# Loading and gating the attention half's output weights before the state-space half's out-projection, in other buffers

## The chip, the cores and the metric

The kernel runs on one core of one Trainium2 chip. The metric is the device time of one launch in microseconds. The kernel before took 1314.43 us (median of three runs, 1313.91 to 1320.89). A change is told from no change here from about 0.5% on, which is 6.6 us.

## The reference, cut to what matters

One decoder layer on 1024 positions of 1024 channels. The input projection is split into two groups of 512 channels: stick-breaking attention (8 heads of 64) and a state-space part. Both are normalised, put side by side, and sent through one output projection:

```python
o = concat([rmsnorm(o_attn, attn_out_g), rmsnorm(o_ssm, ssm_out_g)], axis=-1)
x = x + g1 * (o @ w_out)            # w_out: 1024 x 1024
h = modulate(rmsnorm(x, norm2_g), sh2, sc2)
up = causal_dwconv(h @ ffn_w_up)    # 1024 x 5632, width 3
val, gate = split(up, 2)
x = x + g2 * ((gelu(gate) * val) @ ffn_w_down)
```

The first 512 rows of `w_out` belong to attention, the last 512 to the state-space part.

## The kernel before

Products are done in float32 as three matmuls: each operand is split into a rounded `hi` and a rest `lo`, and hi·hi, hi·lo and lo·hi are summed. The work has four stages: adaLN, norm and input projections with the state-space scan (to about 316 us); attention (to about 579 us); the rest of the output projection and the second norm (to about 690 us); the gated MLP (to the end).

**Attention.** `head` works through the query blocks of a head. A block needs TensorE for the scores (`z`), ScalarE for two sigmoids (`nb`, `sig`), VectorE for a scan over `nb` (L733), GpSimd for a product (`sig`), TensorE for transposes (`wT`), ScalarE and VectorE for the split into `wh` and `wl`, and TensorE for the product with v (`ops`), summed into `oT`. Heads 0 to 5 run one after the other; heads 6 and 7 alternate in groups of two blocks, the last blocks first.

**Fillers.** Beside the heads, two generators are moved on step by step: `ada_fill` (the rest of adaLN, tiles `adps`, `ada_raw`) and `fill`. `marks` holds the places at which `fill` makes a step, as shares of the total work of the heads (a block i counts i + 2, a head 44, all heads 352). The last two heads begin at 0.75, and what is left of `fill` is then run at once. `fill` does, in this order: weight tiles 0 and 1 of the state-space half, the norm statistics of the state-space output (`ssm_stats`, from `oS`), weight tiles 2 and 3, then eight times `ssm_out` (one block of 128 positions), then the four weight tiles of the attention half.

`wout_tile` makes one weight tile: a load of 512 KB into `raw` (tile `woraw`), a VectorE product with the norm gain and `g1row` (the gating), and on GpSimd the rounding to `wohi` and the subtraction to `wolo`. There are four `wohi` and four `wolo` buffers, so that a tile of the attention half can be rounded only when the state-space half has read its own tile for the last time.

`ssm_out` loads a block of x into a tile with the tag `x1`, runs 24 matmuls (two halves of 512 columns, four weight tiles, three products; L806 to L808, tile `wops`), adds the result (L67) and stores the block to `x1_d`. The tag `x1` has one buffer. `woraw`, `ssm_out`'s x and the throw-away output `junk2` of the second norm all use it, so each waits for the one before.

**Tail.** `load_xacc` reads the eight blocks back from `x1_d`: blocks 0 to 3 into the two buffers of the tag `qkraw`, blocks 4 to 7 into the buffer of `oS`. `tail_stats(g)` takes the attention output's statistics as each pair of blocks is complete, and `tail_proj` does the 24 matmuls per block with the attention half's weights, the sum, and the statistics of the second norm. Eight blocks make 192 matmuls. The second norm's transposes (`norm2_t`) and the first MLP products follow.

**Order.** The program gives priorities by its own order. A planner with a cost model then sets each engine's order and takes an instruction when it reckons that its operands and buffers are there. On the chip each engine, and each engine's DMA queue, runs its list in that fixed order and waits at the head of it.

Of the kernel before, what the change touches and what calls it, by code (L numbers as in the profile page):

```python
# [9 lines left out]
F32 = mybir.dt.float32  # L10
# [25 lines left out]
def hybrid_layer_kernel(  # L36
# [17 lines left out]
    act, dve, pool, pe, sp = nc.scalar, nc.vector, nc.gpsimd, nc.tensor, nc.sync  # L54

    def alloc(name, side="left", bufs=1, space=None):
        kw = {} if space is None else {"space": space}
        return tc.alloc_tile_pool(name=name, bufs=bufs, side=side, reuse_waits="tile", **kw)

    def tt(eng, out, a, b, op):  # L60
        eng.tensor_tensor(out=out, in0=a, in1=b, op=op)  # L61
# [4 lines left out]
    def stt(out, a, s, b, op0, op1):  # L66
        dve.scalar_tensor_tensor(out=out, in0=a, scalar=s, in1=b, op0=op0, op1=op1)  # L67
# [108 lines left out]
    def pool_round(o, i):  # L176
        pool.tensor_scalar(out=o, in0=i, scalar1=1.0, scalar2=0.0, op0=MUL, op1=ADD)  # L177
# [37 lines left out]
    for k in range(NK):  # L215
# [4 lines left out]
        raw = ada_raw[k]  # L220
# [177 lines left out]
    for i, (tab, k0) in enumerate(((rot[0], 0), (rot[1], 4))):  # L398
        pool.memset(tab[:, 0, :, 0:1], 1.0)
        pool.memset(tab[:, 1, :, 0:1], 0.0)  # L400
        for k in range(4 - i):
            n = 1 << k
# [215 lines left out]
    for cix in range(2):  # L618
        his, los = load_wchunk(cix)
        for tq in range(4):  # L620
# [14 lines left out]
            for j in range(2):  # L635
# [13 lines left out]
                for r in range(2):  # L649
                    act.dma_start(out=qk_d[cix, r].rearrange("(a p) t -> p a t", p=128)[:, :, t * 128:(t + 1) * 128],  # L650
                                 in_=hl[:, r].bitcast(F32).rearrange("p (a t) -> p a t", t=128))
    smb.release()
    sm.release()
    xq = alloc("qkraw", side="right")
# [31 lines left out]
    osp = alloc("oprep", side="right", bufs=2)  # L686
# [22 lines left out]
    def head(hd, stk, groups, after_tile, after_group):  # L709
        (q1, q2, k1), vt = stk  # L710
        pr, h = divmod(hd, 2)
        for g in groups:
# [42 lines left out]
            after_tile(2 * g + 1)  # L755
            after_group(g)

    def wout_tile(kind, kk, his, los):
        k = kind * 4 + kk
        raw = osp.tile([128, 1024], F32, tag="x1", name="woraw", bufs=1)  # L760
        sp.dma_start(out=raw, in_=w_out[k * 128:(k + 1) * 128, :])
        yield
        stt(raw, raw, outg_sb[:, k:k + 1], g1row, MUL, MUL)
        yield
        hi = wo.tile([128, 1024], F32R, tag="wohi", name="wohi", bufs=4)
        lo = wo.tile([128, 1024], F32R, tag="wolo", name="wolo", bufs=4)
        pool_round(hi, raw)
        tt(pool, lo, raw, hi.bitcast(F32), SUB)
        his.append(hi)
        los.append(lo)  # L770
        yield
# [47 lines left out]
    def ssm_stats(inv):  # L819
        after_v(lambda: sp.dma_start(out=oS, in_=o_d.rearrange("(k p) j c -> p k j c", p=128)))  # L820
        yield
        yield from mix_scale(ap_, psB_new("nps"), oS, range(NT), True, inv)
        yield

    def ssm_out(t, his, los, inv):
        xt_ = osp.tile([128, 1024], F32, tag="x1", name="x1", bufs=1)
        sp.dma_start(out=xt_, in_=x[t * 128:(t + 1) * 128, :])
        yield from out_proj(osp, psB_new, oS, t, True, his, los, xt_, inv)
        sp.dma_start(out=x1_d[t * 128:(t + 1) * 128, :], in_=xt_)

    def fillers():
        his, los = [], []
        inv = small.tile([128, NT], F32, tag="sinv", name="sinv", bufs=1)
        yield from wout_tile(1, 0, his, los)
        yield from wout_tile(1, 1, his, los)
        yield from ssm_stats(inv)
        yield from wout_tile(1, 2, his, los)
        yield from wout_tile(1, 3, his, los)
        for t in range(NT):
            yield from ssm_out(t, his, los, inv[:, t:t + 1])  # L840
        for kk in range(4):
            yield from wout_tile(0, kk, wa_hi, wa_lo)


    marks = [a + (b - a) * j / n for a, b, n in ((0.02, 0.13, 22), (0.13, 0.68, 24), (0.68, 0.75, 12)) for j in range(n)]
    wa_hi, wa_lo = [], []
    ada_fill = ada_back(ap_, ("adaw", "adacc", 2), psB_new, (c32b, mean32b), range(2, 8))
    ada_marks = [0.04 + 0.62 * j / 25 for j in range(25)]
    here = [None]
    fill = fillers()  # L850
    state = {"q": 0, "w": 0}

# [444 lines left out]
```

## Time and profile before

| | us |
|---|---|
| median of three runs | 1314.43 |
| lowest, highest | 1313.91, 1320.89 |
| the profiled execution's own time | 1319.42 |
| its span, first to last instruction | 1317.6 |
| mean granted TensorE clock | 0.961 |

| engine | busy us | share of the span |
|---|---|---|
| TensorE matmul (PE) | 1227.3 | 93% |
| TensorE weight load (PEld) | 996.6 | 76% |
| VectorE (DVE) | 945.9 | 72% |
| ScalarE (ACT) | 602.0 | 46% |
| GpSimd (POOL) | 462.0 | 35% |

The shares are means over stages with different limits. A TensorE that is busy may run matmuls at half the clock, and its ends are modelled: the distance between the starts of successive matmuls says more than the length of one. SP is SyncE, whose queue issues nearly all loads here; a name with q (SPq) is a queue.

### The profile page before, as it was taken

The numbers are of one execution on the slowest core, as the hardware profiler recorded it, in microseconds if no ns is written. First come the engines' busy times: TensorE is split into PE (matmuls) and PEld (weight loads), VectorE is DVE, ScalarE is ACT, GpSimd is POOL, SyncE is SP. The second block draws the span as 40 slices with busy tenths as digits, with TensorE's granted clock in tenths as the row PEclk, the third lists the DMA queues.
The fourth block names the chain that finished last, engine by engine and source line by source line (L and its number), as shares of the span: only waits on it lengthen the run. The fifth ranks groups of instructions, "written<-read, shape, count | busy, mean of one in ns | idle before, by whom it ended". The sixth has DMA issues, their size and how long they took to land.

```text
span 1317.6 us, 17825 instructions
## 1 busy us (share of the span) xinstructions
PE 1227.3 (93%) x6384; PEld 996.6 (76%) x6384; DVE 945.9 (72%) x1443; ACT 602.0 (46%) x1039; POOL 462.0 (35%) x363
## 2 busy tenths in 40 slices
PE   5899989998879898769999999999999999999998
PEld 3677868886667676647877888888888888888887
DVE  4787988644897678867888888888888883345334
ACT  6432332423766466535664555545544553223220
POOL 4553360523763334530016545554554510000000
PEclk9999979998799899879989999999999999999999
DMA  9433563628657877213212222222222155447442
GB/s 345 180 90 92 125 182 76 143 83 257 197 154 210 237 215 197 88 64 134 74 42 95 72 97 78 90 74 96 73 79 90 65 189 187 144 167 249 148 141 102
DMA packets 148791, 178.43 MB, mean 135 GB/s; under 512 B 36304, under 2 KB 103008, under 8 KB 147680
## 3 DMA queue, kind: packets, MB, share of 16 engines
q1 hardware_dynamic: 128640, 157.38, 38.9%
q10 hardware_dynamic: 20064, 19.93, 4.4%
q8 instruction: 50, 0.82, 0.3%
q14 instruction: 37, 0.30, 0.1%
HBM read 135.19 MB, written 40.90 MB: 134 GB/s over the span
## 4 chain that ended last, share of the span: by engine, by line
PE 73%; DVE 14%; DMA 5%; POOL 3%; ACT 3%; issue 2%; SPq 0%; ACTq 0%; DVEq 0%; POOLq 0%
PE dnps L1206 6%; PE dnps L1207 6%; PE dnps L1208 6%; PE up_a L1028 6%; PE up_a L1029 6%; PE up_a L1027 6%; PE up_c L1028 3%; PE up_c L1029 3%; PE up_c L1027 3%; PE wops L806 2%; PE qkvp L563 2%; PE wops L807 2%; PE qkvp L562 2%; PE qkvp L561 2%; PE wops L808 2%
## 5 line engine op out<-in xcount | busy, mean ns | idle before, releaser
L67 DVE SCALAR_TENSOR_TENSOR cv<-up,cols_sb,cv 128x1023 f32<-128x1023 f32 x88 | 145.6, 1655 | 20.5 <-ACT cv L1131 19.8
L61 DVE TENSOR_TENSOR alo<-araw,ahi 128x1024 fp32r<-128x1024 f32 x44 | 53.9, 1225 | 121.3 <-ACT ahi L174 121.2
L61 POOL TENSOR_TENSOR S<-upraw 128x512 f32<-128x512 f32 x40 | 75.6, 1891 | 181.9 <-DMA upraw<-in_w_up_dram 139.5
L1207 PE MATMUL dnps<-wdlo,ahi 128*128 128x512 f32 x352 | 136.9, 389 | 0.0
L1208 PE MATMUL dnps<-wdhi,alo 128*128 128x512 f32 x352 | 136.9, 389 | 0.0
L1206 PE MATMUL dnps<-wdhi,ahi 128*128 128x512 f32 x352 | 134.7, 389 | 0.0
L61 POOL TENSOR_TENSOR sig<-sig,nb 128x127 f32<-128x127 f32 (+3 forms) x64 | 90.8, 1428 | 94.2 <-DVE nb L733 49.3
L61 DVE TENSOR_TENSOR uplo<-S,uphi 128x512 fp32r<-128x512 f32 x80 | 98.1, 1228 | 26.9 <-ACT uphi L174 25.8
L174 ACT ACTIVATE ahi<-araw 128x1024 fp32r<-128x1024 f32 x44 | 46.6, 1060 | 149.2 <-PE dnps L1207 126.6
L733 DVE TENSOR_TENSOR_SCAN nb<-nb 128x128 f32<-128x128 f32 (+3 forms) x64 | 102.9, 1617 | 9.7 <-ACT nb L731 9.3
L61 POOL TENSOR_TENSOR cv<-cv 128x1024 f32<-128x1024 f32 x22 | 54.8, 2489 | 106.2 <-ACT cv L1135 94.9
L174 ACT ACTIVATE uphi<-S 128x512 fp32r<-128x512 f32 x80 | 49.8, 624 | 82.1 <-POOL S L61 67.8
L563 PE MATMUL qkvp<-w_hi,hlo 128*128 128x512 f32 x192 | 77.2, 402 | 0.0
L562 PE MATMUL qkvp<-w_lo,hhi 128*128 128x512 f32 x192 | 77.1, 402 | 0.0
L561 PE MATMUL qkvp<-w_hi,hhi 128*128 128x512 f32 x192 | 77.0, 404 | 0.0
L1208 PEld LDWEIGHTS dnps<-wdhi,alo 128*128 128x128 f32 x352 | 66.1, 188 | 13.8
L1206 PEld LDWEIGHTS dnps<-wdhi,ahi 128*128 128x128 f32 x352 | 66.1, 188 | 13.8
L1207 PEld LDWEIGHTS dnps<-wdlo,ahi 128*128 128x128 f32 x352 | 66.1, 188 | 13.6
L174 ACT ACTIVATE uphi<-upraw 128x512 fp32r<-128x512 f32 x68 | 43.0, 632 | 66.5 <-POOL cv L61 30.9
L61 DVE TENSOR_TENSOR uplo<-upraw,uphi 128x512 fp32r<-128x512 f32 x68 | 68.5, 1009 | 1.6 <-ACT uphi L174 1.6
L806 PE MATMUL wops<-wohi,ohi 128*128 128x512 f32 x128 | 54.1, 427 | 6.8 <-POOL wohi L177 3.7
L740 PE MATMUL wT<-ident,sig 128*128 128x128 f32 x288 | 49.6, 300 | 11.5 <-POOL sig L61 8.6
(334 smaller groups left out, 3416.4 us busy)
## 6 DMA issues: line engine op xcount, KB each, us to landing
upraw<-in_w_up_dram SPq DMA_DIRECT2D x88, 256.0 KB, 3.4
araw<-a_d SPq DMA_DIRECT2D x44, 512.0 KB, 3.3
ada_raw<-in_ada_r_dram SPq DMA_DIRECT2D x64, 256.0 KB, 4.8
a_d<-cv ACTq DMA_DIRECT2D x22, 512.0 KB, 2.8
wdraw<-in_w_down_dram SPq DMA_DIRECT2D x44, 256.0 KB, 3.9
ada_raw<-in_ada_a_dram SPq DMA_DIRECT2D x8, 1024.0 KB, 5.0
qk_d<-hl ACTq DMA_DIRECT2D x32, 256.0 KB, 2.4
q<-qk_d SPq DMA_DIRECT2D x32, 256.0 KB, 6.5
```

The lines of the kernel that those rows point to most:

```text
L61: eng.tensor_tensor(out=out, in0=a, in1=b, op=op)
L67: dve.scalar_tensor_tensor(out=out, in0=a, scalar=s, in1=b, op0=op0, op1=op1)
L174: act.activation(out=o, in_=i, func=AF.Copy)
L561: pe.matmul(o, lhsT=lh, rhs=his[k], start=(k == 0), stop=False)
L562: pe.matmul(o, lhsT=lh, rhs=los[k], start=False, stop=False)
L563: pe.matmul(o, lhsT=ll, rhs=his[k], start=False, stop=(k == NK - 1))
L1027: pe.matmul(ps, lhsT=hi[:, kt, :], rhs=rh, start=(first and kt == 0), stop=False, skip_group_check=True)
L1028: pe.matmul(ps, lhsT=hi[:, kt, :], rhs=rl, start=False, stop=False, skip_group_check=True)
L1029: pe.matmul(ps, lhsT=lo[:, kt, :], rhs=rh, start=False, stop=(kt == 3), skip_group_check=True)
L1206: pe.matmul(o[t], lhsT=hi[:, a], rhs=whi, start=(m == 0), stop=False)
L1207: pe.matmul(o[t], lhsT=hi[:, a], rhs=wlo, start=False, stop=False)
L1208: pe.matmul(o[t], lhsT=lo[:, a], rhs=whi, start=False, stop=(m == NM - 1))
```

## The change

The weight tiles leave the tag `x1`. They are loaded in pairs (1 MB) into the two buffers of `qkraw`, which later hold blocks 0 to 3 of the accumulated x1. The load and the gating of the attention half's four tiles move ahead of the eight `ssm_out`; their rounding stays behind them. The marks follow: after the first 22 steps there are 8 for the loads and gatings (0.13 to 0.20), 24 for `ssm_out` (0.20 to 0.62) and 4 for the roundings (0.62 to 0.68).

```diff
@@ -755,10 +755,14 @@
             after_tile(2 * g + 1)
             after_group(g)
 
+    woraw = {}
+
     def wout_tile(kind, kk, his, los):
         k = kind * 4 + kk
-        raw = osp.tile([128, 1024], F32, tag="x1", name="woraw", bufs=1)
-        sp.dma_start(out=raw, in_=w_out[k * 128:(k + 1) * 128, :])
+        if kk % 2 == 0:
+            woraw[k // 2] = xq.tile([128, 2, 1024], F32, tag="qkraw", name="woraw", bufs=2)
+            sp.dma_start(out=woraw[k // 2], in_=w_out[k * 128:(k + 2) * 128, :].rearrange("(j p) n -> p j n", p=128))
+        raw = woraw[k // 2][:, kk % 2, :]
         yield
         stt(raw, raw, outg_sb[:, k:k + 1], g1row, MUL, MUL)
         yield
@@ -836,13 +840,18 @@
         yield from ssm_stats(inv)
         yield from wout_tile(1, 2, his, los)
         yield from wout_tile(1, 3, his, los)
+        ahead = [wout_tile(0, kk, wa_hi, wa_lo) for kk in range(4)]
+        for w_ in ahead:
+            for _ in range(2):
+                next(w_)
+                yield
         for t in range(NT):
             yield from ssm_out(t, his, los, inv[:, t:t + 1])
-        for kk in range(4):
-            yield from wout_tile(0, kk, wa_hi, wa_lo)
-
-
-    marks = [a + (b - a) * j / n for a, b, n in ((0.02, 0.13, 22), (0.13, 0.68, 24), (0.68, 0.75, 12)) for j in range(n)]
+        for w_ in ahead:
+            yield from w_
+
+
+    marks = [a + (b - a) * j / n for a, b, n in ((0.02, 0.13, 22), (0.13, 0.20, 8), (0.20, 0.62, 24), (0.62, 0.68, 4)) for j in range(n)]
     wa_hi, wa_lo = [], []
     ada_fill = ada_back(ap_, ("adaw", "adacc", 2), psB_new, (c32b, mean32b), range(2, 8))
     ada_marks = [0.04 + 0.62 * j / 25 for j in range(25)]
```

## Rows read from the trace of the kernel before

**Rows 1.** The profile page, parts 1 and 2, whole span: engine busy time, granted clock.

```profile
PE 1227.3 (93%) x6384; PEld 996.6 (76%) x6384; DVE 945.9 (72%) x1443; ACT 602.0 (46%) x1039; POOL 462.0 (35%) x363
...
PEclk9999979998799899879989999999999999999999
```

**Rows 2.** Windows, core 0: stretch, its us, busy us (count) by engine, PEclk, DMA.

```profile
316.00:545.00 229.00, 197.65 (x1430) 158.98 (x1431) 183.70 (x250) 145.48 (x336) 108.91 (x114) 0.91 0.72 200
...
589.00:636.00 47.00, 44.93 (x207) 36.77 (x207) 35.94 (x105) 27.54 (x52) 0.00 (x0) 0.96 0.41 146
...
690.00:1317.60 627.60, 622.22 (x2735) 512.85 (x2734) 430.30 (x398) 263.65 (x366) 200.10 (x98) 1.00 0.35 117
...
545.00:579.20 34.20, 21.50 (x99) 17.57 (x99) 32.33 (x57) 13.13 (x33) 22.82 (x23) 0.74 0.10 31
```

**Rows 3.** Chain that ended last, in time order: start us, us, what; 576 to 594.

```profile
576.35 2.37 POOL wolo L61
...
578.73 3.27 DMA woraw<-in_w_out_dram
...
582.10 1.30 DVE woraw L67
...
584.60 2.36 POOL wolo L61
...
591.15 0.43 PE wops L807
...
594.07 0.23 PE wops L808
```

**Rows 4.** Timeline of TensorE, 584 to 636: start, us, line, tile [idle before].

```profile
584.57 1.22 PE L806 MATMUL wops<-wohi,ohi 128*128 128x512 f32 x2 [3.75 <-POOL wohi L177]
...
587.01 0.80 PE L807 MATMUL wops<-wolo,ohi 128*128 128x512 f32 x1 [1.22 <-POOL wolo L61]
...
635.91 0.39 PE L808 MATMUL wops<-wohi,olo 128*128 128x512 f32 x1
```

**Rows 5.** Windows for instructions on tile wops alone, 545 to 579.2.

```profile
545.00:579.20 34.20, 5.12 (x15) 3.48 (x16) 0.00 (x0) 0.74 0.10 31
```

**Rows 6.** Timeline of VectorE, four instructions between 452 and 579.

```profile
452.82 0.75 DVE L67 SCALAR_TENSOR_TENSOR x<-wops,sinv,x 128x512 f32<-128x512 f32 x1 [7.79 <-PE wops L808]
...
540.89 1.42 DVE L61 TENSOR_TENSOR olo<-oT,ohi 128x512 fp32r<-128x512 f32 x2
...
576.50 2.22 DVE L67 SCALAR_TENSOR_TENSOR ainv<-rs_h,ainv 128x2 f32<-128x2 f32 x1
...
578.75 0.42 DVE L61 TENSOR_TENSOR oT<-ops,otmp 64x256 f32<-64x256 f32 x1
```

**Rows 7.** Tile woraw: min/median/max ns, first and last start, shapes.

```profile
L67 DVE SCALAR_TENSOR_TENSOR woraw<-woraw,cols_sb,g1row x8: 1264/1278/1289, 318.6 to 582.1; 128x1024 f32<-128x1024 f32 x8
L177 POOL TENSOR_SCALAR wohi<-woraw x8: 1041/1203/2481, 325.7 to 583.5; 128x1024 fp32r<-128x1024 f32 x8
L61 POOL TENSOR_TENSOR wolo<-woraw,wohi x8: 2353/2531/4185, 329.4 to 584.6; 128x1024 fp32r<-128x1024 f32 x8
```

**Rows 8.** Tile x of the state-space out-projection, same columns.

```profile
L67 DVE SCALAR_TENSOR_TENSOR x<-wops,sinv,x x16: 725/751/752, 394.9 to 535.4; 128x512 f32<-128x512 f32 x16
```

**Rows 9.** Timeline of SyncE, first two loads of x at line 827.

```profile
386.01 0.49 SPq L827 DMA_DIRECT2D x<-in_x_dram  x1
...
399.81 0.34 SPq L827 DMA_DIRECT2D x<-in_x_dram  x1
```

**Rows 10.** DMA issues by tile: count, KB each, median us to landing.

```profile
ada_raw<-in_ada_a_dram SPq DMA_DIRECT2D x8, 1024.0 KB, 5.0
...
woraw<-in_w_out_dram SPq DMA_DIRECT2D x8, 512.0 KB, 3.5
```

**Rows 11.** SyncE's own waits, 310 to 600: total us, times, longest.

```profile
SPq L829 <- DVE x L67: 21.3, 6, 5.4
...
SPq L761 <- POOL wolo L61: 20.8, 5, 7.8
```

## The prediction, made before the result was known

> **What bounds the kernel now.** I read the engine shares first, then windows by stage, then the chain of waits, then each engine's timeline around the longest gap in the chain. TensorE is busy for 93% of the span, so only a stretch where it is not, or where it runs slow, can give time back [rows 1]. From 690 us to the end it is busy for 622 of 628 us at full clock: nothing can be gained there, and whatever is gained earlier is carried to the end unchanged [rows 2]. In attention proper (316 to 545) it is busy for 86% and VectorE for 80%, with neither saturated. In the stretch from 545 to 579 VectorE is busy for 32.3 of 34.2 us and bounds the heads, while TensorE works for 21.5 us at a mean granted clock of 0.74. The second norm's stretch (589 to 636) is TensorE's again, 44.9 of 47 us.
>
> Between these two lies the gap. The chain of waits passes from GpSimd's `wolo` (576.35) to a load of `woraw` (578.73), VectorE's gating (582.10) and the next `wolo` (584.60) [rows 3]. That is the attention half's last weight tiles passing one at a time through a single buffer: a tile is loaded only when the one before has been split. TensorE sits idle for 3.75 us until a `wohi` and then for 1.22 us until the `wolo`, and what it does next runs at half the clock: at 591 a `wops` matmul takes 0.43 us in the chain, at 594 it takes 0.23 [rows 3, 4]. The heads themselves are over by then: the last piece of `oT` starts at 578.75 [rows 6].
>
> **The change part by part.**
>
> *Late load, gating and rounding removed from the tail.* The `hi` and `lo` parts of the first two blocks of attention output that the tail needs exist from 540.89 + 1.42 = 542.3 [rows 6]; before, their products wait for weights. Of 192 tail matmuls only 15 have started by 579.2 [rows 5]. By 589.1 it is 24, and the last starts at 635.91 [rows 4]. Three terms go:
> - Waits of TensorE: 3.75 + 1.22 = 5.0 us.
> - Half clock: I count 16 `wops` from 579.2 until the clock is back shortly after 592 (9 of the first block, 7 of the second), each 0.43 - 0.23 = 0.20 us too long: 3.2 us.
> - Matmuls moved ahead of the heads' end. With weights there, the first two blocks (48 matmuls) can run beside the heads. That is 33 more than now, 33 x 0.23 = 7.6 us at full clock. TensorE has 34.2 - 21.5 = 12.7 us idle in that window, so they fit. I take two blocks and no more, because the next pair needs statistics that come late in the heads.
>
> Sum: 5.0 + 3.2 + 7.6 = 15.8 us. Next to bind is TensorE itself with the rest of the 192 and the norm's transposes. VectorE, busy for 35.9 of 47 us in 589 to 636, must follow a start 16 us earlier, and has had room for it.
>
> *Are the weights there in time?* The rounding must wait for the state-space half's last use of its weights. Its last sum starts at 535.4 [rows 8]. Four roundings at the median are 4 x (1.20 + 2.53) = 14.9 us on GpSimd [rows 7], so even without any earlier end they are there by about 551, with 28 us left for 11 us of matmuls. I expect them earlier: the first x is loaded at 386.01 because its buffer was held by the weight tiles, and from then the shortest round of load, sum and store is 399.81 - 386.01 = 13.8 us [rows 9]. Eight such rounds are 110 us, so 496 is the early end.
>
> *Moved loads.* Eight loads of 512 KB become four of 1 MB. The nearest row of that size lands in 5.0 us, against 3.5 us for one tile [rows 10]. The first gating can thus come 1.5 us later. Other filler work covers this, and I take 0 (bounds 0 and 1.5). SyncE issues four instructions fewer. In its queue the attention half's two loads move past `ssm_out`'s loads and stores, the heads' q, k and v and the adaLN rows, and wait there for the roundings of the state-space tiles. Waits of that sort now cost its queue 20.8 us in five [rows 11]; with two buffers there are two such places instead, so I take 0 (bounds -2 and +4, half of the longest, 7.8). The reads of x1 for blocks 0 to 3 now wait for `qkraw` until the rounding is done. The queue behind them holds the last heads' loads; the tail needs those blocks only after 589. Cost 0.
>
> *Moved gating.* Four VectorE instructions at 1.28 us are 5.1 us [rows 7], before paid at 543 to 583, three of the four inside the VectorE-bound stretch, and now paid among heads 1 and 2. The work is the same, in a stretch with idle time on VectorE (229 - 183.7 = 45 us over all of it). I take 0, bounds -3.8 (the three come back at the heads' end) and +5.1.
>
> *Denser `ssm_out`.* The eight blocks get 0.42 of the heads' work instead of 0.55, about their shortest round. One stall there, VectorE idle for 7.79 us until `wops` in the middle of head 4 [rows 6], follows three reads of x1 issued ahead of adaLN rows; those reads move. I take 0, bounds -7.8 and the price of the last rival below.
>
> The span was 1317.6; less 15.8 it is 1301.8. With the 1.8 us that lie around it the profiled execution would take 1303.6. That execution (1319.42) was 5.0 us above the median of the runs, so against the median I forecast 1314.4 - 15.8 = 1298.6. The case's own range is 1293 to 1304, from the bounds just given.
>
> **A rule against the change.** At 576.50 a VectorE instruction on 256 elements takes 2.22 us [rows 6], longer than one on 65,536 (0.75) [rows 8], and GpSimd's `wolo` covers just that time (576.35, 2.37 long). `wohi` and `wolo` themselves range from 1.04 to 2.48 and from 2.35 to 4.19 us [rows 7]. The Trainium skill (SBUF — State Buffer, section Who interferes with whom) says that VectorE with two operands in SBUF and a reading GpSimd take turns at one port pair, and that whoever comes second stands still for a whole instruction. The trace agrees, and by this rule roundings that move beside the scans are not free; what that would make of the time is the second rival, worked out from the rows.
>
> **The rivals.**
>
> 1. *The weights come late all the same.* If the planner puts the roundings behind the last heads, or `ssm_out` ends no sooner, only the one-at-a-time chain goes: waits and half clock, 5.0 + 3.2 = 8.2 us, giving 1306. For it: the marks at 0.62 stand behind `ssm_out`'s release of `wohi`, which now comes at 535. Against it: the 28 us left over above. 15%.
> 2. *The heads get longer by what the tail saves.* Two of the four pairs of rounding (575 to 579 and 583 to 587) now lie beside a VectorE with little to do. Beside the scans they can block it for 2 x (1.04 + 2.35) = 6.8 us. The sums of two tail blocks that also move into the heads are four of 0.75, 3.0 us, and two splits at 0.71, 1.4 us. In all 11.2 us on an engine with 1.9 us of slack there, less the gatings that leave (3.8): 7.4. With the early gatings at their upper bound (5.1), 12.5 go and 3.3 are left: 1311. Against it: the roundings should lie in head 5, where VectorE has gaps. 15%.
> 3. *The stall in head 4 goes too,* as no read of x1 stands in front of the adaLN rows there: 15.8 + 7.8 = 23.6, giving 1291. Against it: the reads meet the loads of the last heads instead. 13%.
> 4. *Slower: SyncE's queue stands in front of the adaLN rows.* With rounds at their shortest length each store of a block waits at the head of SyncE's queue for VectorE's sum, and adaLN rows and head loads wait behind it; TensorE takes these in order. Now such stores hold the queue for 21.3 us in six, 3.55 each [rows 11]. If all eight rounds pass this on to the heads, 8 x 3.55 = 28.4 us are lost against 15.8 gained: 1327. It decides from 2.8 us a round on (8 x 2.8 = 15.8 + 6.6). Against it: the heads' own loads are issued a head ahead. 7%.
>
> **How the numbers follow.** Forecast 50%, rivals 15, 15, 13 and 7%. A measurement of this kernel tells a difference from about 0.5%, 6.6 us, on: faster means below 1307.9, slower above 1321.0. The forecast and rival 3 are faster, and four fifths of rival 1 (it lies 1.6 us inside the border): 0.50 + 0.13 + 0.12 = 0.75. Rival 2 and the rest of rival 1 are no change, 0.18. Rival 4 is slower, 0.07. The range runs from 1288, a few us below rival 3, to 1311, which takes in rival 1 and half of rival 2; rival 4 and the rest stay out.
>
> **What would show it.** Right: in the changed trace all eight `wolo` end before 551, TensorE does not wait for `wohi` or `wolo` after 545, the granted clock stays full from the heads' end through the last `wops`, 40 or more `wops` of the tail have started when the last `oT` is written, and the time from that `oT` to the last `wops` is some 41 us instead of 57. The heads' end stays within a few us of 579. Wrong: roundings between the last scans (rival 1, or 2 if the last `oT` is later by as much as the tail is shorter), or TensorE idle at `adps` behind stores of x1 in heads 1 to 5 (rival 4). A stage after the last `wops` that is longer than before would refute that the gain is carried to the end.

## The result, and the profile after

| | before | after |
|---|---|---|
| median, us (6 runs each, side by side) | 1319.04 | 1331.68 |
| lowest, highest | 1313.91, 1323.76 | 1330.21, 1339.60 |
| ratio of the times, 95% interval | 1 | 1.0121 [1.0091, 1.0151] |
| profiled execution, its span | 1319.42, 1317.6 | 1338.74, 1337.0 |

The change makes the kernel 1.2% slower, and the interval lies clear of 1; forecast was 1.2% faster. The profiled executions differ by 19.3 us, the medians by 12.6: after's profiled execution lies 7.1 us above its own median, so some 7 of the 19.3 belong to that one execution and not to the kernel.

To find the place I cut the span at five events: the first scan of attention (VectorE, L733), the end of head 1's and of head 5's widest scan, the start of the last `wops`, and the end.

| stretch | before | after | difference |
|---|---|---|---|
| up to the first scan | 316.8 | 320.6 | +3.7 |
| heads 0 and 1 | 53.8 | 68.2 | +14.4 |
| heads 2 to 5 | 131.8 | 150.1 | +18.2 |
| heads 6 and 7, and the tail to the last `wops` | 133.5 | 113.6 | -19.8 |
| the rest | 681.7 | 684.6 | +2.8 |

On these figures the tail gains even more than forecast, and three stretches that I had costed at nothing take it back nearly twice. Part of the -19.8 and of the +18.2 is the same work in another place, as shown below. The page of after, busy time by engine and the granted clock in 40 slices, shows no engine with more work than in [rows 1] but for 1.5 us on TensorE; what changes is where TensorE stands and where its clock dips.

```profile
PE 1228.8 (92%) x6384; PEld 998.3 (75%) x6384; DVE 945.1 (71%) x1443; ACT 601.2 (45%) x1039; POOL 458.5 (34%) x363
...
PEclk9999999989679988799998999999999999999999
```

The windows of after: stretch, its us, busy us (count) for PE, PEld, DVE, ACT, POOL, granted clock, DMA share, GB/s. Heads 0 and 1, heads 2 to 5, the end of the heads, the tail, the MLP:

```profile
320.00:389.00 69.00, 46.25 (x287) 34.92 (x286) 55.13 (x64) 42.20 (x93) 41.26 (x34) 0.72 0.70 196
389.00:539.00 150.00, 132.01 (x936) 105.87 (x936) 100.11 (x152) 76.52 (x182) 46.84 (x65) 0.89 0.64 178
599.00:615.10 16.10, 15.78 (x79) 13.12 (x80) 11.38 (x28) 6.62 (x13) 0.13 (x1) 1.00 0.13 53
615.10:652.80 37.70, 36.23 (x176) 29.82 (x175) 31.98 (x99) 24.41 (x46) 0.00 (x0) 1.00 0.47 159
707.00:1337.00 630.00, 622.44 (x2725) 512.79 (x2723) 428.49 (x397) 262.58 (x365) 198.68 (x98) 0.99 0.35 117
```

The first two stretches in the kernel before, same columns:

```profile
316.00:371.00 55.00, 41.20 (x250) 32.87 (x250) 46.28 (x52) 40.32 (x90) 40.31 (x31) 0.78 0.81 220
371.00:503.00 132.00, 117.08 (x901) 92.83 (x901) 104.42 (x158) 78.70 (x185) 53.57 (x68) 0.95 0.74 209
```

The reader is to see that heads 0 and 1 hold about the same work on GpSimd (41.3 against 40.3 us) in 14 us more, that TensorE is busy for 46 of 69 us there, with more matmuls at a lower clock (0.72 against 0.78), and that from 599 to 652.8 the clock is full and TensorE has next to no gap. After 707 TensorE is as full as in [rows 2].

**The tail, as forecast.** The last piece of `oT` and the last `wops` of after, and the windows of `wops` alone just before that `oT`:

```profile
615.12 0.42 DVE L61 TENSOR_TENSOR oT<-ops,otmp 64x256 f32<-64x256 f32 x1
```

```profile
652.42 0.39 PE L812 MATMUL wops<-wohi,olo 128*128 128x512 f32 x1
```

```profile
599.00:615.10 16.10, 13.17 (x55) 10.08 (x56) 3.00 (x4) 1.00 0.13 53
```

From the last `oT` to the last `wops` it takes 652.42 - 615.12 = 37.3 us, against 57.2 before [rows 4, 6] and 41 forecast; 55 of the tail's matmuls have started by then (before 15 [rows 5], forecast 40 or more).

How much of the 19.8 us is a gain is shown by the windows of `wops` alone (stretch, its us, busy us and count for PE, PEld, DVE, granted clock, DMA share, GB/s) in heads 2 to 5 and from there to the last `oT`: first before, then after, then the later stretch alone in e8, an experiment below:

```profile
370.60:502.40 131.80, 37.80 (x144) 28.00 (x144) 8.92 (x12) 0.95 0.74 209
502.40:578.70 76.30, 16.59 (x62) 11.76 (x62) 2.97 (x4) 0.87 0.33 97
```

```profile
388.70:538.80 150.10, 55.75 (x187) 41.01 (x188) 11.23 (x15) 0.89 0.64 178
538.80:615.10 76.30, 14.68 (x62) 10.98 (x61) 3.75 (x5) 0.89 0.24 78
```

```profile
501.70:587.20 85.50, 26.72 (x103) 19.94 (x104) 5.99 (x8) 0.86 0.39 114
```

Heads 6 and 7 take 76.3 us in both kernels, with 62 `wops` each: in after, 42 state-space matmuls (9.7 us at 0.23) have left them for heads 2 to 5, and about as many of the tail have taken their place. In e8 none has left (144 by the end of head 5, as before), and heads 6 and 7 take 9.2 us more; in e5, with 55 `wops`, they take 74.4. The count is not all of it, as f1 takes 85.5 with 67. From the last `oT` to the last `wops` it takes 37.2 or 37.3 us in every kernel below that has the weights in `qkraw`, 19.9 less than before; net of what the heads pay for it, the gain in e8 is 10.7 us.

**The beginning, where it is lost.** The weight tiles `woraw`, `wohi`, `wolo` of after (min/median/max ns, first and last start) answer to [rows 7]:

```profile
L67 DVE SCALAR_TENSOR_TENSOR woraw<-woraw,cols_sb,g1row x8: 1268/1282/1897, 285.8 to 364.6; 128x1024 f32<-128x1024 f32 x8
L177 POOL TENSOR_SCALAR wohi<-woraw x8: 1043/1876/2787, 325.1 to 545.9; 128x1024 fp32r<-128x1024 f32 x8
L61 POOL TENSOR_TENSOR wolo<-woraw,wohi x8: 2361/2440/4326, 334.5 to 562.7; 128x1024 fp32r<-128x1024 f32 x8
L764 SPq DMA_DIRECT2D woraw<-in_w_out_dram x4: 378/410/467, 280.4 to 349.4; - x4
```

The first gating stands at 285.8 us, not at 318.6: 33 us earlier, among the input projections. It was not the sharing of the one buffer `x1` that had kept the first load back, but the buffer's place: its pool takes memory that the input projections use until they end, as the waits show. SyncE's waits of before (us, times, longest), and of after:

```profile
SPq L761 <- PE qkvp L563: 3.2, 1, 3.2
```

```profile
SPq L764 <- DVE gt L61: 22.1, 1, 22.1
SPq L831 <- PE qkvp L563: 2.2, 1, 2.2
```

Before, the first load of `woraw` (L761) waits for the last projection matmuls (`qkvp`). In after x (L831), now the first in `x1`, waits for the same, and the pair in `qkraw` (L764) waits for `gt` of the state-space part and goes out at 280.39, 34 us earlier. VectorE among the projections (start us, us, instruction, idle time before it), and the first matmul that waits on it:

```profile
285.76 2.61 DVE L67 SCALAR_TENSOR_TENSOR woraw<-woraw,cols_sb,g1row 128x1024 f32<-128x1024 f32 x2 [3.73 <-DMA woraw<-in_w_out_dram]
289.25 2.48 DVE L67 SCALAR_TENSOR_TENSOR woraw<-woraw,cols_sb,g1row 128x1024 f32<-128x1024 f32 x2 [0.88 <-DMA woraw<-in_w_out_dram]
292.64 1.29 DVE L61 TENSOR_TENSOR vt<-qkvp,vt 128x512 fp32r<-128x512 f32 x2 [0.91 <-ACT vt L672]
```

```profile
293.48 0.77 PE L561 MATMUL qkvp<-w_hi,hhi 128*128 128x512 f32 x1 [5.19 <-DVE vt L61]
```

VectorE stands for 3.73 and 0.88 us in front of the two loads with the splits of v behind it, and TensorE waits for 5.19 us for such a split (`vt`). Then GpSimd and TensorE in head 0 of after:

```profile
323.49 1.63 POOL L61 TENSOR_TENSOR sig<-sig,nb 128x383 f32<-128x383 f32 x1 [0.96 <-DVE nb L733]
325.09 8.37 POOL L177 TENSOR_SCALAR wohi<-woraw 128x1024 fp32r<-128x1024 f32 x4
333.43 1.08 POOL L61 TENSOR_TENSOR sig<-sig,nb 128x511 f32<-128x511 f32 x1
334.48 4.68 POOL L61 TENSOR_TENSOR wolo<-woraw,wohi 128x1024 fp32r<-128x1024 f32 x2
339.11 3.31 POOL L61 TENSOR_TENSOR sig<-sig,nb 128x639 f32<-128x639 f32 x1
342.38 4.81 POOL L61 TENSOR_TENSOR wolo<-woraw,wohi 128x1024 fp32r<-128x1024 f32 x2
347.15 6.61 POOL L61 TENSOR_TENSOR sig<-sig,nb 128x767 f32<-128x767 f32 x3
```

```profile
334.57 1.11 PE L740 MATMUL wT<-ident,sig 128*128 128x128 f32 x4 [4.46 <-POOL sig L61]
```

With all four tiles gated by 292 us, the planner gives GpSimd four `wohi` in a row (8.37 us) and the `wolo` in pairs (4.68 and 4.81). The product `sig`, without which a block's transposes can't start, stands behind them, and TensorE waits 4.46 us at 334.57. Before, the same stretch has one `wohi` (325.68, 2.48 us) and one `wolo` (329.40, 4.18 us), each with products between.

The loss shows a head later. By the ends of the widest scans head 0 takes 20.7 us (before 18.9) and head 1 47.4 (34.8). TensorE's waits for `sig` are no longer in sum than before (6.2 us in four, before 6.8 in five); what differs is that the last three products of head 0 begin at 347.15, 26.6 us after the first scan (before 16.7), and that TensorE, with 4 to 6 us of work in each 10, stays at the lower clock for thirty us (before, the same three windows stand at 0.67, 0.84 and 0.66):

```profile
330.00:340.00 10.00, 4.31 (x18) 3.40 (x17) 5.91 (x3) 3.14 (x7) 10.00 (x6) 0.51 1.09 332
340.00:350.00 10.00, 5.88 (x34) 4.48 (x34) 6.71 (x9) 5.74 (x10) 10.00 (x5) 0.50 0.90 235
350.00:360.00 10.00, 6.04 (x25) 5.22 (x26) 8.36 (x10) 5.45 (x9) 5.06 (x6) 0.50 0.46 157
```

How the 12.6 us of head 1 divide between late products and the clock is not worked out.

**Heads 2 to 5.** By the windows above TensorE is busy for 132.0 of 150.0 us there, before for 117.1 of 132.0: 15 of the 18 us are busy time, from 42 more `wops` and a clock of 0.89 instead of 0.95, and 3 are idle. VectorE's waits there (us in all, times, longest) show loads that it hardly waited for before (0.5 us for x in all; the profile puts one wait of the sum down to the load of k, which the sum does not read):

```profile
DVE x L67 <- PE wops L812: 18.7, 9, 6.4
...
DVE x L67 <- DMA k<-qk_d: 6.0, 1, 6.0
...
DVE x L67 <- DMA x<-in_x_dram: 4.8, 2, 3.1
```

and the chain that ended last passes through long loads. The shares of these heads in the chain by line, of after and of before, and the loads among after's pieces (start us, us, what):

```profile
by line: DMA ada_raw<-in_ada_r_dram 20.1%; PE wops L810 9.4%; DMA x<-in_x_dram 8.5%; PE wops L811 8.3%; PE wops L812 8.0%; PE adps L589 5.6%; PE wT L740 5.4%; PE ops L751 4.9%; PE ops L750 4.7%; DMA k<-qk_d 4.5%; PE z L727 4.1%; PE z L728 3
...
460.50 8.40 DMA x<-in_x_dram
...
478.56 6.65 DMA ada_raw<-in_ada_r_dram
...
504.90 6.76 DMA k<-qk_d
...
524.86 9.22 DMA ada_raw<-in_ada_r_dram
```

```profile
by line: DMA ada_raw<-in_ada_r_dram 13.7%; DVE nb L733 8.9%; PE wops L806 8.2%; PE wops L807 7.7%; PE wops L808 7.2%; PE wT L740 6.0%; PE adps L589 5.5%; issue 4.8%; DMA x<-in_x_dram 4.6%; PE ops L750 4.4%; PE z L727 4.0%; PE ops L751 4.0%;
```

In after the chain lies for (20.1 + 8.5 + 4.5)% of 150.1 = 50 us in loads, before for (13.7 + 4.6)% of 131.8 = 24; and for 38.6 us instead of 30.4 in `wops`, of which 42 more have started by the end of head 5. These are only moved, and are part of what the last table row but one shows as the tail's gain.

### The profile page after: what moved, and what is told of

It reads as the page before. It is cut to its first block, busy times and chain, and to the rows that moved or that the text cites. A ratio compares the mean times of both kernels' runs of the same rounds, so it can differ in the third digit from the quotient of the medians.

```text
span 1337.0 us, 17821 instructions
## 1 busy us (share of the span) xinstructions
PE 1228.8 (92%) x6384; PEld 998.3 (75%) x6384; DVE 945.1 (71%) x1443; ACT 601.2 (45%) x1039; POOL 458.5 (34%) x363
## 4 chain that ended last, share of the span: by engine, by line
PE 68%; DVE 13%; DMA 9%; issue 3%; POOL 2%; ACT 2%; SPq 1%; ACTq 0%; DVEq 0%; POOLq 0%
PE dnps L1216 6%; PE dnps L1215 6%; PE dnps L1217 6%; PE up_a L1036 5%; PE up_a L1038 5%; PE up_a L1037 5%; PE up_c L1038 3%; PE up_c L1036 3%; PE up_c L1037 3%; DMA ada_raw<-in_ada_r_dram 2%; PE wops L810 2%; PE wops L811 2%; PE wops L812 2%; PE qkvp L563 2%; PE qkvp L562 2%
## 5 line engine op out<-in xcount | busy, mean ns | idle before, releaser
L61 POOL TENSOR_TENSOR sig<-sig,nb 128x127 f32<-128x127 f32 (+3 forms) x64 | 87.0, 1367 | 108.8 <-DVE nb L733 73.7
L733 DVE TENSOR_TENSOR_SCAN nb<-nb 128x128 f32<-128x128 f32 (+3 forms) x64 | 100.3, 1578 | 11.3 <-ACT nb L731 11.1
L1217 PEld LDWEIGHTS dnps<-wdhi,alo 128*128 128x128 f32 x352 | 66.1, 188 | 13.7
L731 ACT ACTIVATE nb<-z 128x512 f32<-128x512 f32 (+2 forms) x96 | 48.3, 504 | 35.8 <-PE z L728 12.8
```

The source lines that it names most:

```text
L733: dve.tensor_tensor_scan(out=nb[:, 0:n][:, ::-1], data0=nb[:, 0:n][:, ::-1], data1=nb[:, 0:n][:, ::-1], initial=1.0, op0=MUL, op1=ALU.bypass)
L1217: pe.matmul(o[t], lhsT=lo[:, a], rhs=whi, start=False, stop=(m == NM - 1))
```

## The experiments

Five theories are told apart. **T1**: the freed buffers let the state-space weight tiles go early, and their roundings stand before the first heads' products. **S**: the paired loads themselves, issued during the projections, hold up the start. **T2**: the out-projection's rounds stand too close. **X**: in heads 2 to 5 the single buffer of x makes VectorE wait for loads. **L**: what heads 2 to 5 take is an accident of the order that comes out of each edit. Two expectations name a further rival, G: the moved gating and the statistics on VectorE cost heads 0 and 1. All differences below are against the same profiled execution of before, in the five stretches of the table above; the medians are against runs of before on the same chip. Each kernel has one profiled execution, which can lie some us off its median (after's and b's 7 above, e3's 7 below), so single differences of a few us between two rows are not read. The last column but two counts the `wops` that have started by the end of head 5, each 0.23 us of work that has left heads 6 and 7.

| kernel | start | heads 0, 1 | heads 2 to 5 | 6, 7, tail | rest | `wops` by head 5 (before 144) | median | ratio [95%] |
|---|---|---|---|---|---|---|---|---|
| after | +3.7 | +14.4 | +18.2 | -19.8 | +2.8 | 186 | 1331.68 | 1.0121 [1.0091, 1.0151] |
| a_wide | +6.0 | +14.4 | +4.1 | -18.3 | +0.7 | 168 | 1321.59 | 1.0024 [1.0004, 1.0044] |
| b_ssm_x1 | +9.4 | +2.5 | -3.4 | -13.2 | +0.3 | 163 | 1307.67 | 0.9915 [0.9888, 0.9941] |
| c_both | +4.3 | +1.9 | +1.6 | -11.4 | +1.1 | 153 | 1315.51 | 0.9990 [0.9972, 1.0008] |
| d_before_dense | -0.1 | -0.2 | +2.8 | -8.4 | +0.6 | 163 | 1314.30 | 0.9977 [0.9952, 1.0003] |
| e1_b_held | -1.5 | +1.4 | +14.3 | -12.0 | +2.0 | 168 | 1321.11 | 1.0028 [1.0006, 1.0050] |
| e6_a_held | -4.1 | -1.8 | +9.2 | -13.1 | 0.0 | 163 | 1312.59 | 0.9961 [0.9931, 0.9990] |
| e3_pool_tied | +5.5 | -0.1 | +3.4 | -12.1 | +0.3 | 168 | 1323.80 | 1.0047 [1.0021, 1.0073] |
| e5_buf_only | +4.2 | +14.2 | +12.7 | -21.8 | +3.0 | 192 | 1330.16 | 1.0101 [1.0065, 1.0136] |
| e8_held_wide | -2.6 | -1.7 | +3.6 | -10.7 | -0.1 | 144 | 1308.21 | 0.9937 [0.9902, 0.9973] |
| e9_held_tied | -4.0 | -1.7 | +9.6 | -11.9 | +0.2 | 163 | 1313.69 | 0.9967 [0.9943, 0.9991] |
| e12_held_shift | -4.2 | -1.7 | +20.1 | -12.7 | +1.8 | 156 | 1322.08 | 1.0037 [1.0012, 1.0063] |
| f1_shift_half | -0.3 | +2.1 | +11.9 | -10.7 | -0.1 | 180 | 1326.40 | 1.0056 [1.0022, 1.0091] |
| f3_e6_half | +0.2 | +2.1 | +12.2 | -16.4 | +0.1 | 178 | 1318.51 | 1.0030 [1.0008, 1.0052] |
| f2_wide_half | -1.6 | +2.1 | +12.9 | -13.5 | +0.1 | 159 | 1319.23 | 1.0007 [0.9984, 1.0030] |

**The state-space tiles back in their one buffer, and the old spacing: a, b, c, d.**

a_wide, after with the places of before for the rounds:

```diff
-    marks = [... ((0.02, 0.13, 22), (0.13, 0.20, 8), (0.20, 0.62, 24), (0.62, 0.68, 4)) ...]
+    marks = [... ((0.02, 0.13, 30), (0.13, 0.68, 24), (0.68, 0.75, 4)) ...]
```

> The changed kernel with the marks of before for the state-space out-projection (0.13 to 0.68; the gating steps ahead of 0.13, the roundings at 0.68 to 0.75). Theory T1, burst: without the single buffer the planner puts loads, gatings and eight roundings of the state-space weights in one block at the start of attention, and this costs all that was lost (about 18 us in the projection's end and heads 0 and 1): this run stays within 5 us of the changed kernel. Theory T2, density: the out-projection in 0.42 of the heads' work instead of 0.55 stops VectorE and TensorE for late loads of x in heads 3 to 5 (about 18 us): this run is about 18 us faster than the changed kernel, near 1313.

b_ssm_x1, after with the state-space half's raw tiles in `x1` again; c_both is a and b together:

```diff
+        if kind:
+            raw = osp.tile([128, 1024], F32, tag="x1", name="wsraw", bufs=1)
+            sp.dma_start(out=raw, in_=w_out[k * 128:(k + 1) * 128, :])
+        else:
+...
```

> The changed kernel, but the state-space half's four weight tiles are loaded one at a time through the buffer with the tag x1, as before; only the attention half's are in qkraw. T1: the roundings are spread again, heads 0 and 1 end within 5 us of the kernel before, and the time falls by about 18 us to 1313. T2: it stays within 5 us of the changed kernel, 1331.

> Both edits of the two runs above. If T1 and T2 each hold half of the loss, their sum gives back some 32 us of which the tail's gain of 17 is left against the kernel before: near 1302. If only one holds, no faster than the better of the two runs above, near 1313.

d_before_dense, the kernel before with after's spacing of the rounds:

```diff
-    marks = [... ((0.02, 0.13, 22), (0.13, 0.68, 24), (0.68, 0.75, 12)) ...]
+    marks = [... ((0.02, 0.13, 22), (0.20, 0.62, 24), (0.62, 0.75, 12)) ...]
```

> The kernel before with one edit: the marks of the state-space out-projection at 0.20 to 0.62 and of the attention half's weight tiles at 0.62 to 0.75. T2: slower than before by about 18 us, near 1337, with VectorE waiting for loads of x. T1: within 5 us of before.

With the tiles of the state-space half in `x1`, heads 0 and 1 lose 2.5 and 1.9 us instead of 14.4, whatever the spacing (b, c), and with all tiles in `qkraw` they lose 14.4 whatever the spacing (a). T1's place is confirmed. T2 alone is refuted: before with close rounds is no slower. The wide spacing helps after by ten microseconds, which neither T1 (5 at most) nor T2 (18) had expected of a, but takes eight from b (c), so its sign hangs on what stands around it. The start is late in all kernels that still load into `qkraw` early (a, b, c) and in none without (d).

**The loads held: e1, e6.** In b and in after, the paired load is queued on SyncE behind the last store of v:

```diff
-                sp.dma_start(out=woraw[k // 2], in_=...)
+                after_v(lambda: sp.dma_start(out=woraw[k // 2], in_=...))
```

> The kernel with the state-space tiles one at a time through x1 (the second run above), and the attention half's two paired loads queued on SyncE behind the last store of v. Theory S: loads that go out during the projections cost the start of attention its 9.4 us there (first scan at 326.2 instead of 316.8), since VectorE and the stores of v stand behind them. Then the first scan comes at 317 to 318 and the time falls by 7 to 9 us to about 1299. Rival: the two loads only move into the head loads, heads 0 and 1 lose what the start gains, and the time stays at 1307.

> The changed kernel with its paired loads queued on SyncE behind the last store of v, so none goes out during the projections. Theory S alone: 3.7 us of the start come back, 1328. Theory T1 (the block of roundings): the rest of the loss stays, heads 0 and 1 still 10 us or more over before. Rival: gating and rounding come later and are spread by that alone; then heads 0 and 1 are within 5 us of before and the time is near 1315.

S holds: the start goes from +9.4 to -1.5 (e1) and from +3.7 to -4.1 (e6). In e6 the first gating moves to 333.8 us, and heads 0 and 1 go from +14.4 to -1.8 with it, though nothing else was undone: the tiles come spread out again. e6 is after with one edit and is 0.4% faster than before, 0.9961 [0.9931, 0.9990]; T1's expectation, that heads 0 and 1 keep their loss, is missed, and its rival came true. Over all sixteen profiles the first scan lies at 312.7 to 317.0 us where no load goes into `qkraw` during the projections, and at 320.6 to 326.2 where one does. e1 is a miss: b with its start mended is slower than b, as heads 2 to 5 lose 14.3 us that b didn't.

**GpSimd's order alone: e3.** After's loads and buffers, but a step of `fill` may not be taken up before the block's product on GpSimd either:

```diff
-                tt(pool, sig[:, 0:n - 1], sig[:, 0:n - 1], nb[:, 1:n], MUL)
+                psig[0] = pool.tensor_tensor(out=sig[:, 0:n - 1], in0=sig[:, 0:n - 1], in1=nb[:, 1:n], op=MUL)
...
-                with tc.issue_after(here[0].ins):
+                with tc.issue_after(here[0].ins), tc.issue_after(psig[0].ins):
                     next(fill, None)
```

> The changed kernel with one edit: GpSimd's filler instructions are queued behind the current block's product of sig, as TensorE's are behind its scores, so that the roundings follow the marks. T1 (GpSimd's block of eight roundings stops the heads): heads 0 and 1 lose 5 us at most instead of 14.4, and the time falls by about 10 us to 1321 or less. Rival G (it is the moved gating and the statistics on VectorE): heads 0 and 1 keep 10 us or more of the loss and the time stays at 1331.

GpSimd in head 0 of e3 (start us, us, instruction):

```profile
329.14 1.05 POOL L177 TENSOR_SCALAR wohi<-woraw 128x1024 fp32r<-128x1024 f32 x1
330.15 1.33 POOL L735 TENSOR_TENSOR sig<-sig,nb 128x639 f32<-128x639 f32 x1
331.44 1.06 POOL L177 TENSOR_SCALAR wohi<-woraw 128x1024 fp32r<-128x1024 f32 x1
332.45 7.84 POOL L61 TENSOR_TENSOR wolo<-woraw,wohi 128x1024 fp32r<-128x1024 f32 x2
340.26 7.32 POOL L735 TENSOR_TENSOR sig<-sig,nb 128x767 f32<-128x767 f32 x3
```

The roundings stand among the products, `wolo` still in a pair, and heads 0 and 1 lose nothing (-0.1). The start stays late (+5.5), as S has it. So the 14.4 us hang on GpSimd's order and not on the loads, and G falls too: the attention half's gatings still stand at 359 to 377 us. The median of 1323.8 misses the 1321 that T1 had asked for. The profiled execution of 1316 is the fastest of ten, so for the whole time the median counts.

**The buffers alone: e5.** After without the attention half's tiles ahead:

```diff
-        ahead = [wout_tile(0, kk, wa_hi, wa_lo) for kk in range(4)]
-        for w_ in ahead:
-            for _ in range(2):
-                next(w_)
-                yield
...
-        for w_ in ahead:
-            yield from w_
+        for kk in range(4):
+            yield from wout_tile(0, kk, wa_hi, wa_lo)
...
-    marks = [... (0.13, 0.20, 8), (0.20, 0.62, 24), (0.62, 0.68, 4)) ...]
+    marks = [... (0.20, 0.62, 24), (0.62, 0.75, 12)) ...]
```

> The changed kernel with the buffers alone: all weight tiles in pairs in qkraw, but the attention half's loaded, gated and rounded behind the state-space out-projection again (marks 0.62 to 0.75). T1: heads 0 and 1 lose 10 us or more as in the changed kernel, since the block of roundings is that of the state-space tiles. Rival G: without the moved gating the loss there falls under 5 us. The tail's gain should stay within 5 us of the changed kernel's 19.8, since two tiles are loaded at a time.

Same loss (+14.2 in heads 0 and 1, median 1330) and the same tail gain (-21.8): the raw tiles' two free buffers alone bring both. The planner gates the attention half's tiles at 358 to 365 us in either kernel, so the written move ahead does next to nothing.

**Out of heads 2 to 5: e8, e9, e12, and the half tiles f1, f2, f3.** All hold the loads as e6 does. e8 has a's spacing, e9 e3's tie, and e12 shifts the rounds by 0.01 of the heads' work:

```diff
-    marks = [... (0.20, 0.62, 24), (0.62, 0.68, 4)) ...]
+    marks = [... (0.21, 0.63, 24), (0.63, 0.68, 4)) ...]
```

> The changed kernel with its paired loads held behind the last store of v (the run at 1312.6) and the wide marks for the state-space out-projection (0.13 to 0.68; gatings ahead of 0.13, roundings at 0.68 to 0.75). T2 in the smaller form that the runs left (the dense marks make VectorE wait for x, 7.4 us there against 0.5 before): waits for x under 4 us, heads 2 to 5 within 4 us of before instead of +9.2, time near 1306. Rival L (the planner's order shifts the middle heads by some us whatever the marks): heads 2 to 5 stay at +7 or more and the time is 1311 or more.

> The held kernel (1312.6) with GpSimd's fillers queued behind the current block's sig product. T1: holding the loads has already taken the block of roundings apart, so the tie adds nothing in heads 0 and 1 (within 3 us) and the time stays within 5 us of 1312.6. Rival: the tie takes a further 5 us or more, 1307 or less.

> The held kernel (1312.6) with the marks of the state-space out-projection moved by 0.01 (0.21 to 0.63), which changes neither its density nor any buffer. L (the order alone is worth several us): the time moves by 4 us or more either way, in heads 2 to 5 and the tail. Otherwise it is within 3 us of 1312.6, and differences of 5 us between these kernels may be read as their edits.

e8 is the best of these, 1308.2, and meets what T2 in its smaller form had asked of it (waits for x 2.7 us, heads 2 to 5 at +3.6); of its 5.6 us under e6 in these heads, 19 `wops` fewer are 4.4. e9 equals e6. e12 is the surprise: 9.5 us in the median and 11 in heads 2 to 5 for a shift of a hundredth. Ten of the 11 are in head 5 alone (43.3 us by the widest scans, e6 33.2). VectorE waits in it for 14.1 us for x, 12.6 of them in head 5:

```profile
DVE x L67 <- DMA x<-in_x_dram: 14.1, 4, 6.7
```

That made X. f1, f3 and f2 are e12, e6 and e8 with x in two half tiles, each loaded, summed and stored by itself, which doubles the loads and stores of x in SyncE's queue. `junk2`, which shares the tag, becomes bfloat16 so as to fit:

```diff
-        xt_ = osp.tile([128, 1024], F32, tag="x1", name="x1", bufs=1)
...
+        for n in range(2):
+            xh.append(osp.tile([128, 512], F32, tag="x1", name="x1", bufs=2))
...
```

> The held kernel with the marks moved by 0.01 (1322), with x of the state-space out-projection in two half tiles of 512 columns in two buffers of the same total size: the first half's buffer is free, and its next load out, half a round earlier. Theory X (the middle heads lose time because VectorE stands at a sum whose x has not landed, after a single buffer came free late): waits for x in heads 2 to 5 under 5 us instead of 14.1, those heads at +8 or less instead of +20, time 1313 or less. Rival L (the order's luck, of which the waits for x are only one form): the waits fall and the heads do not get shorter by more than 5 us.

> The held kernel (1312.6) with the same half tiles of x. X: waits for x under 4 us instead of 7.4, heads 2 to 5 at +5 or less instead of +9.2, time near 1308. With both this and the run above at about the same time, the 9.5 us that the shift of 0.01 cost was the wait for x. L: the two still differ by 6 us or more.

> The held kernel with wide marks (1308.2) with the same half tiles. VectorE waits only 2.7 us for x there, so X expects little: within 3 us of 1308.2. If it is faster by 5 us or more, the half tiles help in another way than by the wait for x, and the two runs above don't show X.

The waits for x go from 14.1, 7.4 and 2.7 us to 0, 0 and 0.6, and the time doesn't follow: heads 2 to 5 stand at +12 to +13 in all three, 8 us less than e12 but 3 more than e6 and 9 more than e8, and no median is better. f1 falls between its two expectations (X asked for +8 or less, L for a gain of 5 at most), with 24 more `wops` in these heads than e12 (5.5 us); so in e12 the waits for x may well be the loss. As the cause in all kernels X is not borne out: f3 and f2 take 10 and 11 us more than X had given. The half tiles are not a clean trial of it either, as they also cost heads 0 and 1 4 us, where no x is awaited. Where x is there, TensorE waits longer for adaLN rows, which come through the same queue (`adps`: 8.1, 7.5 and 10.7 us in heads 2 to 5; e12, e6 and e8 2.1, 2.8 and 6.5). L is what is left, and it is a name for scatter, not a mechanism.

## Why the prediction was wrong

**Right in the place, too large in the size: the tail.** All three terms came, and show behind the last `oT` (37.3 us, forecast 41). TensorE waits for no `wohi` or `wolo` after 545, and the clock is full through the last `wops`. Two signs failed: the last `wolo` starts at 562.7 instead of ending before 551, and the heads end at 615, not within a few us of 579. The weights are still early enough, as the first tail matmul starts at 599.8. The third term, "33 x 0.23 = 7.6 us", took it that these matmuls fit into TensorE's idle time at no cost to the heads. In e8, where no state-space matmuls left them, heads 6 and 7 get 9.2 us longer with 41 more `wops` (9.4 us), so 10.7 of the forecast 15.8 are left; in after the 42 matmuls that moved to heads 2 to 5 hide it. That the forecast's size was reached, 19.8 us, is thus luck: by these counts about half of it is work that other stretches had taken over. The gain is carried to the end but for 2.8 us in the rest: at 710 to 760 us TensorE is busy for 46.8 of 50 at a clock of 0.93, at the same place before for 49.2 at 1.00 (in the other runs the rest is -0.1 to +3.0).

**Wrong: "Moved loads ... I take 0 (bounds 0 and 1.5)".** This is the step that failed. I costed what the four larger loads are, how long they take to land and where they stand in SyncE's queue, for the attention half, and under "Moved gating" its four gatings, which did come in head 1 (358.1 to 366.5). I did not ask what the buffer of `x1` had kept back for the state-space half. The marks tie only TensorE's filler instructions to their place; loads, gatings and roundings the planner takes as soon as it reckons buffers and operands there. Before, the buffer was their brake: the first load held until the projections ended, then one 512 KB tile at a time, the first gated at 318.6. With two buffers in memory that comes free earlier the first gating comes 33 us earlier and not 1.5 later. The sum had 0 for the state-space tiles, which the argument never listed as moved; they cost 3.7 us at the start (S; e6 against after) and 14.4 in heads 0 and 1 (T1; b, e3 and e6 each take it away). 15.8 forecast against 18.1 lost: this step alone takes the whole gain, and what heads 2 to 5 lose beyond the moved work comes on top.

**Wrong in size: "Denser `ssm_out` ... I take 0, bounds -7.8 and the price of the last rival".** Heads 2 to 5 lose 18.2 us in the profiled execution. 9.7 are the 42 moved matmuls and up to 7 that execution's distance from its median; what remains is small in after and not settled. Density alone isn't it (d), the waits for x alone aren't (f2, f3), the tie isn't (e9), and the hold leaves 9.2 (e6), of which 19 moved matmuls are 4.4.

Two slips in the working change no verdict. The bounds given add up to 1285.0 to 1309.2, not 1293 to 1304, even without the price of the last rival. And two of the four gatings, not three, lay inside the stretch from 545 to 579 (they start at 543.2, 559.5, 573.9 and 582.1).

**The rivals.** Rivals 1 and 3 fell. Rival 2 had the engine, roundings on GpSimd beside the scans, and put it in heads 6 and 7 instead of 0 and 1; and the price went with products that queue behind roundings, not with scans that stand still for them. Its other half, that the heads get longer by the tail's work that moves into them, is borne out by e8 (9.2 us). [rows 7] had roundings of 1.04 to 2.48 us; after has 1.04 to 2.79, and `wolo` up to 4.33. The Trainium skill (SBUF — State Buffer, section Who interferes with whom) has the one that comes second at the shared port pair stand for the whole of the other's instruction. The trace agrees for single instructions: the widest scan at 337.41 takes 3.90 us and the one at 386.44, with no rounding beside it, 2.28; the `wolo` beside the first ends 1.75 us after that scan starts. No run here shows the 14.4 us to be that, and e3, with as many roundings in the same heads and no loss, speaks against it.

Rival 4 had the sign and nearly the median, 1327, but its price isn't there. SyncE's own waits in after (us, times, longest):

```profile
SPq L579 <- PE adps L589: 61.9, 28, 10.9
SPq L833 <- DVE x L67: 21.2, 6, 6.3
SPq L579 <- DMA ada_raw<-in_ada_r_dram: 20.8, 13, 3.7
```

Stores of x wait for 21.2 us in six, as before (21.3 in six, [rows 11]), where the rival asked for 28.4 more passed on to the heads. Its place has something in it, though: loads take 26 us more of the chain in heads 2 to 5, 12 of them the adaLN rows.

**What stays open.** Which order makes heads 2 to 5 short. The medians of the seven kernels with all paired loads held, which differ in the spacing of the rounds, a tie or a half tile, lie between 1308 and 1326, and no wait named in the traces goes along with it through all runs: the loads' share of the chain is 50 us in after and 48 in e5, the long ones, but 26 in e12, the longest, and 38 in c, one of the short ones. The moved `wops` explain part of it in after and e5 (11 us of e5's 12.7), but not e12, which has fewer of them than e6. e6 and e12 were measured on two chips, each beside its own before. More buffers for the adaLN rows, or another queue for x, weren't tried.

**The better version.** b_ssm_x1, the state-space half's tiles in `x1` and the attention half's in `qkraw`, takes 1307.67 us, 0.9915 [0.9888, 0.9941] of before, and e8 1308.21, 0.9937 [0.9902, 0.9973]: faster than both kernels. Some 11 and 9 of the forecast 15.8 us can thus be had. In e8, whose profiled execution is its median, the ledger finds them in the tail (-10.7); b's profiled execution lies 7 us above its median, so where its 11 us come from is not shown.

## What to carry to other kernels

A buffer is also a brake, by who shares it and by whose memory it takes over. Before a tile is given another one, list every instruction that had waited for the old one, on every engine, and ask where a planner will put it when it no longer waits; then hold the load on purpose, as e6 does with one edit. When work moves from one stretch into another, count it in both before the difference is called a gain. And where an order is planned, an edit of a few microseconds is measured with its order: try it in two or three neighbouring places before a gain or a loss below one per cent is put down to it.

## What the runs showed that was not expected

- A shift of the filler's marks by 0.01 of the heads' work changed the median by 9.5 us (1312.6 to 1322.1, ratios to before [0.9931, 0.9990] and [1.0012, 1.0063]): more than most edits here.
- A gap on the bottleneck can be a wait that does good. The Trainium skill (Perfetto Trace Analysis, section Optimization Strategy) says that a gap that repeats can mean that there is no room for the next tile. For the tail the trace agrees: the waits of 3.75 and 1.22 us go with the two buffers. From the start to head 1 the same two buffers cost 18.1 us.
- The price of the four `wohi` in a row is more than TensorE's wait of 4.46 us behind them. For thirty us, from 330 to 360, the granted clock of after is 0.50 or 0.51, the level of 1.2 GHz, while TensorE stands for 4 to 6 of each 10 us. Matmuls that start in such stretches take about twice as long (`wops` 0.43 us against 0.23 [rows 3]).
